# A layer's closing stage put under a written engine order, with two smaller moves of one product and one weight split

## The chip, the cores and the metric

The kernel runs on one core of a Trainium2 chip. The time is the device time of one execution in microseconds; the kernel before takes 1223.93 us (median of 3 runs, 1222.23 to 1228.37).

## What is computed

One layer of a hybrid attention and convolution backbone over 640 tokens of width 1024 (128 context tokens and 512 latent tokens, all float32). The part that matters here is the feed-forward half, with D_FF = 2816:

```python
def conv_ffn(u, p):
    up = dwconv3(u @ p["w_up"], p["conv_ffn"])
    g, val = jnp.split(up, 2, axis=-1)
    return (jax.nn.silu(g) * val) @ p["w_down"]

def trunk_layer(h, ada, p, rope_tabs, ctx_k, ctx_v):
    ...
    h = h + g1 * rms_norm(mo, p["g_post1"])
    u = rms_norm(h, p["g_pre2"]) * (1 + sc2) + sh2
    h = h + g2 * rms_norm(conv_ffn(u, p), p["g_post2"])
    return h, k, v
```

`dwconv3` is a three-tap convolution along the tokens, so an activation tile needs a whole row of tokens. The rest of the layer (modulation, attention, gated convolution, output projection) comes ahead and is the same in both kernels.

## The kernel before, in words

**Products in three parts.** Every large product keeps float32 accuracy by cutting both operands into a high part (a ScalarE copy to a rounded type, `S.activation(..., AF.Copy)`) and a low part (a VectorE subtraction). `mm3` then issues three TensorE matmuls: high by high, high by low, low by high. So every weight tile of 128x1024 costs one ScalarE copy and one VectorE subtraction before TensorE can use it: `split` (L149, L150) for tiles that come through `next_unit`, `hi_of`/`lo_of` (L872, L876) for the w_up tiles, `down_hi`/`down_lo` (L985, L989) for the first 512 columns of w_down, which have one buffer `WD`, and `act_hi`/`act_lo` (L967, L971) for the activations.

**w_up in pairs.** The 2816 columns of each half of w_up are 22 pairs j of 128 columns (NJ = 22). Pairs 0 and 1 are done plainly by `plain(j, tok, i, step)`, 12 matmuls of 322 columns each. Pairs 2 to 21 are done by `strassen(j)` in seven products of 12 matmuls: A11, A12, S2, S1, S3, S4, A22. Two banks of the accumulator memory hold a pair; A22 writes again into the bank of which `added(cv[:, HALF:], j, "p5", 0)` (L931, tile `C`) reads the earlier content, so A22 waits for that VectorE addition.

**Activations, three pairs behind.** While pair j is multiplied, pair j - 3 goes through `tap_mid` (ScalarE, L948), two `taps_out` (VectorE, L953, two instructions each), `silu` (ScalarE), `gated` (VectorE, L962, which also stores the product tile to the DRAM tensor `actd`), `act_hi` and `act_lo`. The high and low parts live in a ring of four tiles (`ACTa`, `ACTb`).

**w_down, first half of the columns.** `down(k)` multiplies activation tile k by its rows of w_down for output columns 0 to 511, 15 matmuls of 512 columns (five token tiles, three matmuls each) in five banks. It runs one pair of w_up later than the activation is made, between S1 and S3. `WD` holds two k at a time and is filled on odd pairs behind S3; the first fill stands in pair 3.

**w_down, second half.** Columns 512 to 1023 need all 22 activation tiles again. Tiles 18 to 21 are still in the ring (`again(i, ts)`, three matmuls per token tile); tiles 0 to 17 are read back from `actd` into `AFB` (eight slots, `act_fetch`) and cut again by `act_of` into `AHB` (L1288) and `ALB` (L1289). The w_down tiles for it (list `rest`) come through `next_unit`. `finish(0, t)` squares and scales the first half of the columns, `finish(1, t)` the second, adds the two sums of squares, takes the inverse root on GpSimd (L1304) and writes the output.

**What sets the order.** From the end of the mixer on, the order of TensorE, ScalarE and VectorE is the order in which the program is written (`manual_schedule`, entered in the ExitStack `fixed`). `fixed.close()` ends this ahead of the loop over tiles 0 to 17; what stands behind it is ordered by a scheduler, which may put its instructions ahead of ones that were written earlier. The queue of SyncE, which issues nearly all DMAs, is ordered by the scheduler throughout. Where the text speaks of a queue, it means an engine's instructions in the order of the built program.

The two remaining places: `turn2(4, hf)` (L822) transposes the last normalised token tile `TX`, and `modulated(4, hf)` scales it into the right-hand operands `B12` and `B22` of the second half of the tokens; `B11` and `B21`, the first half, are complete by then.

Of the kernel before, what the change touches and what calls it, by code (L numbers as in the profile page):

```python
# [11 lines left out]
F32 = mybir.dt.float32  # L12
F32R = mybir.dt.float32r
AF = mybir.ActivationFunctionType
ALU = mybir.AluOpType
AX = mybir.AxisListType

D = 1024
# [3 lines left out]
NT = 5  # L22
# [49 lines left out]
def trunk_layer(ctx, tc, x_prompt, x_sample, cache_k, cache_v, c, c_ctx, w_ada, b_ada, g_pre1, g_post1, g_pre2,  # L72
# [71 lines left out]
    def split(raw):  # L144

        n = raw.shape[1]
        hi = wp.tile([128, 1024], F32R, tag="whi", name=nm("whi"), bufs=3)
        lo = wp.tile([128, 1024], F32R, tag="wlo", name=nm("wlo"), bufs=3)
        S.activation(hi[:, :n], raw, AF.Copy)  # L149
        V.tensor_tensor(out=lo[:, :n], in0=raw, in1=hi[:, :n].bitcast(F32), op=ALU.subtract)  # L150
        return hi, lo

    def fetch(i):
        while len(state["raw"]) < min(i, len(units)):
            w, k0, nk, c0, n = units[len(state["raw"])]
            raw = raw_tile()
            nc.sync.dma_start(raw[:, :nk * n].rearrange("p (k c) -> p k c", c=n),
                              w[k0 * 128:(k0 + nk) * 128, c0:c0 + n].rearrange("(k p) c -> p k c", p=128))
            state["raw"].append(raw)

    def next_unit():
        i = state["next"]
        state["next"] += 1
        fetch(i + 3)
        while len(state["cut"]) < min(i + 2, len(units)):
            w, k0, nk, c0, n = units[len(state["cut"])]
            raw = state["raw"][len(state["cut"])]
            state["cut"].append(Unit(split(raw[:, :nk * n]), n))
        return state["cut"][i]

    def mm3(out, ah, al, bh, bl, start, stop):
# [647 lines left out]
    def turn2(t, hf):  # L819
        p = turned[t, hf] = bank((t, 5 if t == 0 else t - 1)[hf])  # L820
        for k in range(4):
            PE.transpose(p[:, k * 128:(k + 1) * 128], TX[:, t % 2, (4 * hf + k) * 128:(4 * hf + k + 1) * 128], ident)  # L822
# [72 lines left out]
    def plain(j, tok, i, step):  # L895

        if step == 0:
            plain_out[j, tok, i] = bank(PLAIN_BANKS[j, tok, i])[:, 0:HALF]
        block(plain_out[j, tok, i], (j, i), step, f"B{step + 1}{tok + 1}", step == 0, step == 1)
# [46 lines left out]
    def tap_mid(j, i):  # L946
        y, o = acts(j)[0][i], i * NJ + j
        S.activation(y, crows(j)[i][:, 1:1 + NACT], AF.Copy, scale=cffn[:, 44 + o:45 + o])  # L948

    def taps_out(j, i):  # L950
        y, o = acts(j)[0][i], i * NJ + j
        for d in (0, 2):
            V.scalar_tensor_tensor(out=y, in0=crows(j)[i][:, d:d + NACT], scalar=cffn[:, 44 * d + o:44 * d + o + 1], in1=y,  # L953
                                   op0=ALU.mult, op1=ALU.add)

    def silu(j):
        y = acts(j)[0][0]
        S.activation(y, y, AF.Silu)

    def gated(j):  # L960
        ys = acts(j)[0]
        V.tensor_tensor(out=ys[0], in0=ys[0], in1=ys[1], op=ALU.mult)  # L962
        nc.sync.dma_start(actd[j], ys[0])

    def act_hi(j):
        ys, parts = acts(j)
        S.activation(parts[0], ys[0], AF.Copy)  # L967

    def act_lo(j):
        ys, parts = acts(j)  # L970
        V.tensor_tensor(out=parts[1], in0=ys[0], in1=parts[0].bitcast(F32), op=ALU.subtract)  # L971
# [15 lines left out]
    def down_lo(q):  # L987
        hi, lo = (room["wd"][:, i, :] for i in range(2))
        V.tensor_tensor(out=lo, in0=dn["raw"][q], in1=hi.bitcast(F32), op=ALU.subtract)  # L989
# [12 lines left out]
    def strassen(j):  # L1002

        f, nxt = j - FLAG, j + 1 if j + 1 < NJ else None
        g = NJ - FLAG if nxt is None else None
        cg, cv = crows(j)
        pair[j] = tuple(bank(n)[:, 0:HALF] for n in BANKS[j])
        if j > NPLAIN:
            last_copy(j - 1)
        else:  # L1010
            plain_copy(1, 1, 1)
        if f >= 0:
            tap_mid(f, 0)
        lo_of((j, 1))
        product(j, "A11")

        copied(j, "p1", 0)
        if f >= 0:
            tap_mid(f, 1)
            taps_out(f, 0)  # L1020
        product(j, "A12")

        hi_of((j, 2), left(j, 2))
        added(cg[:, 0:HALF], j, "p1", 1)
        lo_of((j, 2))
        product(j, "S2")

        copied(j, "u2", 0)
        if f >= 0:
            silu(f)  # L1030
            taps_out(f, 1)
        product(j, "S1")

        copied(j, "p5", 1)
        hi_of((j, 3), left(j, 3))
        if f >= 0:
            gated(f)
        lo_of((j, 3))
        if nxt:
            adds = sums(nxt)  # L1040
            adds[0]()
        if g:
            tap_mid(g, 0)
            tap_mid(g, 1)
        if j >= DLAG:
            down(j - DLAG)
        product(j, "S3")

        if nxt:
            pair_load(j + 2)  # L1050
            hi_of((nxt, 0), left(nxt, 0))
            lo_of((nxt, 0))
        q = (j - DLAG + 1) // 2
        if j >= DLAG - 1 and (j - DLAG) % 2 == 1:
            down_hi(q)
            down_lo(q)
            down_load(q + 2 if q else 1)
            if q == 0:
                down_load(2)
        added(cv[:, HALF:], j, "p5", 0)  # L1060
        if nxt:
            adds[1]()
        if f >= 0:
            act_hi(f)
        if g:
            taps_out(g, 0)
            silu(g)
        product(j, "S4")

        if nxt:  # L1070
            hi_of((nxt, 1), left(nxt, 1))
        added(cg[:, HALF:], j, "u2", 1)
        if nxt:
            adds[2]()
        if f >= 0:
            act_lo(f)
        if g:
            taps_out(g, 1)
            gated(g)
            act_hi(g)  # L1080
            act_lo(g)
        product(j, "A22")

    def last_copy(j):
        S.activation(crows(j)[1][:, 0:HALF], pair[j][0], AF.Copy)
# [122 lines left out]
    normed(4)  # L1208
    right_hi("B12", "12", 0, 192)
    plain(0, 0, 1, 1)  # L1210
    turn2(4, 0)
    modulated(4, 0)
    right_lo("B22", "22", 0, 192)
# [1 line left out]
    modulated(4, 1)  # L1215
    pair_load(2)
    pair_load(3)
    plain(1, 0, 0, 0)
    right_lo("B12", "12", 0, 192)
    right_hi("B12", "12", 192, HALF)  # L1220
    right_hi("B22", "22", 192, HALF)
# [42 lines left out]
    down_load(0)  # L1264
    plain(1, 1, 1, 1)
    for j in range(NPLAIN, NJ):
        strassen(j)


# [23 lines left out]
    def finish(n, t, pm):  # L1293
        row = 1 if t == 0 else 0
        cs = slice(n * 512, (n + 1) * 512)
        S.activation(JK[:, t % 2, :], pm, AF.Square, accum_out=ssqs[:, t, n:n + 1])
        V.tensor_tensor(out=EX[:, t, cs], in0=pm, in1=G2[:, row, cs], op=ALU.mult)
        first, second = ssqs[:, t, 0:1], ssqs[:, t, 1:2]
        if n == 0:
            V.tensor_scalar(out=first, in0=first, scalar1=D * EPS, scalar2=None, op0=ALU.add)  # L1300
            nc.sync.dma_start(room["h"][:, t, :], hd[t])
            return
        V.tensor_tensor(out=second, in0=second, in1=first, op=ALU.add)  # L1303
        G.tensor_tensor(out=second, in0=second, in1=mhalf[:, 0:1], op=ALU.pow)  # L1304
        for i in range(2):
            cs = slice(i * 512, (i + 1) * 512)
            V.scalar_tensor_tensor(out=EX[:, t, cs], in0=EX[:, t, cs], scalar=second, in1=room["h"][:, t, cs], op0=ALU.mult, op1=ALU.add)
            nc.sync.dma_start(yrows(t)[:, cs], EX[:, t, cs])

    def ending(f):  # L1310

        tap_mid(f, 0)
        tap_mid(f, 1)
        taps_out(f, 0)
        silu(f)
        taps_out(f, 1)
        gated(f)
        act_hi(f)
        act_lo(f)


    units += rest
    pms = [bank(b) for b in RING if b not in BANKS[NJ - 1]]
    us = []

# [3 lines left out]
        for t in ts:  # L1329
            wd_step(pms[t], t, acts(k)[1], us[i // 2].at(i % 2), i == 0, False)  # L1330

    last_copy(NJ - 1)
    ending(NJ - 2)
    fetch(state["next"] + 3)
    down(NJ - 4)
    down(NJ - 3)
    us.append(next_unit())
    pms += [bank(b) for b in BANKS[NJ - 1]]
    again(0, range(3))
    down_hi(NJ // 2 - 1)  # L1340
    down_lo(NJ // 2 - 1)
    again(1, range(3))
    ending(NJ - 1)
    down(NJ - 2)
    us.append(next_unit())
    again(2, range(3))
    act_fetch(5)
    for row in range(2):
        bload(G2[:, row, :], 3, row)
    down(NJ - 1)  # L1350
    again(3, range(3))
    room["h"] = region(ra, "r3", [NT, D], F32, "HX")
    for t in range(NT):
        finish(0, t, dn["pms"][t])
        if t == 1:
            pms += [bank(b) for b in DBANKS[:2]]
            for i in range(4):
                again(i, (3, 4))
    fixed.close()
    NU, tail, av = NJ // 2 - 2, 3, {}  # L1360
    for q in range(NU):
        us.append(next_unit())
        for k in (2 * q, 2 * q + 1):
# [4 lines left out]
    for t in range(NT):  # L1368
        for k in range(2 * (NU - tail), 2 * NU):
            wd_step(pms[t], t, av[k], us[2 + k // 2].at(k % 2), False, k == 2 * NU - 1)  # L1370
        finish(1, t, pms[t])


# [27 lines left out]
```

## Time and profile before

| what | value |
|---|---|
| runs | 1222.23, 1223.93, 1228.37 us |
| the profiled execution, its own time | 1227.19 us |
| its span, first to last instruction | 1225.4 us |
| TensorE busy | 1188.6 us (97%) |
| VectorE, ScalarE, GpSimd busy | 685.1, 526.6, 151.8 us |
| DMA | 130.39 MB, 106 GB/s over the span |

A row of the timeline gives the start, the duration, the engine, the line and the operation, out<-in by tile names; `[x <-E]` behind it says that the engine stood idle for x us before and what ended that. A matmul row's duration runs to the end of its pipeline, so that matmuls which follow each other overlap; the distance between two starts is what one costs. In the view of stretches the column PEclk is the share of full speed that the TensorE clock was granted.

### The profile page before, as it was taken

Reading aid. Unit: us, or ns where it says so; the run is one execution under the profiler, and the core shown is the slowest. Engines: PE = TensorE matmul, PEld = TensorE weight load, DVE = VectorE, ACT = ScalarE, POOL = GpSimd, SP = SyncE. Lnnn points to the kernel's source line nnn. Section 1 sums busy time; section 2 is a strip of 40 time slices with the busy share of each in tenths; the row PEclk is TensorE's granted clock in tenths of the full one; section 3 lists DMA queues with packets and bytes.
Section 4 is the critical chain, followed back from the end, with each engine's and each line's share of the span. In section 5 each row is a group of like instructions: output and inputs, shape, how many; then the busy total and the mean of one; then the engine's idle time right before and its main releaser. Section 6 shows DMA issues by size and latency. Waiting matters only on the chain. (4 is left out here: it accounts for less than half of the span.)

```text
span 1225.4 us, 19707 instructions
## 1 busy us (share of the span) xinstructions
PE 1188.6 (97%) x8109; PEld 1089.1 (89%) x8109; DVE 685.1 (56%) x1091; ACT 526.6 (43%) x896; POOL 151.8 (12%) x188
## 2 busy tenths in 40 slices
PE   6999999999999999999999999989999999997997
PEld 5788888877999999999999987989999999995886
DVE  4486666555122234343333336787888888887443
ACT  4276666665221122222222226555555555555331
POOL 1045556554000000000000003000000000000001
PEclk7998999999999999999999999999999999998999
DMA  8834223144122222222222263333333333316622
GB/s 260 247 112 118 74 70 104 36 121 122 55 70 80 75 70 83 73 70 86 70 70 86 72 202 122 121 100 89 108 105 95 104 100 108 108 57 256 210 63 86
DMA packets 180936, 130.39 MB, mean 106 GB/s; under 512 B 6322, under 2 KB 162542, under 8 KB 180846
## 3 DMA queue, kind: packets, MB, share of 16 engines
q1 hardware_dynamic: 180062, 128.83, 35.0%
q8 instruction: 64, 1.05, 0.4%
q10 hardware_dynamic: 784, 0.30, 0.1%
q14 instruction: 26, 0.21, 0.1%
HBM read 116.34 MB, written 12.77 MB: 105 GB/s over the span
## 5 line engine op out<-in xcount | busy, mean ns | idle before, releaser
L885 PE MATMUL b<-ZB,whi 128*128 128x322 f32 x1024 | 228.2, 310 | 0.0
L149 ACT ACTIVATE whi<-raw 128x1024 fp32r<-128x1024 f32 (+1 forms) x87 | 88.5, 1018 | 317.4 <-PE s L173 166.9
L172 PE MATMUL s<-UH,whi 128*128 128x320 f32 x640 | 198.2, 310 | 0.5 <-ACT PT L588 0.5
L174 PE MATMUL s<-UH,wlo 128*128 128x320 f32 x640 | 197.2, 308 | 0.0
L173 PE MATMUL s<-UL,whi 128*128 128x320 f32 x640 | 197.2, 308 | 0.0
L150 DVE TENSOR_TENSOR wlo<-raw,whi 128x1024 fp32r<-128x1024 f32 (+1 forms) x87 | 102.5, 1179 | 162.4 <-ACT whi L149 160.3
L885 PEld LDWEIGHTS b<-ZB,whi 128*128 128x128 f32 x1024 | 173.7, 189 | 1.6
L885 PE MATMUL b<-ZB,wlo 128*128 128x322 f32 x512 | 159.1, 311 | 0.0
L172 PEld LDWEIGHTS s<-UH,whi 128*128 128x128 f32 x640 | 120.1, 188 | 1.5 <-issue 0.8
L174 PEld LDWEIGHTS s<-UH,wlo 128*128 128x128 f32 x640 | 120.1, 188 | 0.4 <-issue 0.4
L173 PEld LDWEIGHTS s<-UL,whi 128*128 128x128 f32 x640 | 120.1, 188 | 0.0
L885 PEld LDWEIGHTS b<-ZB,wlo 128*128 128x128 f32 x512 | 96.2, 188 | 0.0
L563 POOL TENSOR_TENSOR pr<-pr,sm 128x640 f32<-128x640 f32 x64 | 80.1, 1256 | 67.2 <-DVE sm L561 57.7
L953 DVE SCALAR_TENSOR_TENSOR Y<-C,cffn,Y 128x642 f32<-128x642 f32 x88 | 77.8, 886 | 3.5 <-ACT Y L948 1.8
L872 ACT ACTIVATE whi<-SUM 128x1024 fp32r<-128x1024 f32 x40 | 42.2, 1055 | 59.8 <-PE b L885 53.9
L172 PE MATMUL s<-whi,UH 128*128 128x256 f32 (+1 forms) x200 | 64.5, 322 | 2.6 <-ACT UH L355 1.7
L560 ACT ACTIVATE pr<-s,mx,rq 128x640 f32<-128x640 f32 x64 | 56.6, 885 | 16.5 <-DVE mx L557 14.5
L555 DVE TENSOR_REDUCE mx<-s 128x1 f32<-128x640 f32 x64 | 52.4, 821 | 19.9 <-PE s L552 19.5
L173 PE MATMUL s<-wlo,UH 128*128 128x256 f32 (+1 forms) x200 | 63.1, 316 | 0.0
L174 PE MATMUL s<-whi,UL 128*128 128x256 f32 (+1 forms) x200 | 61.3, 319 | 0.0
L1304 POOL TENSOR_TENSOR ssqs<-ssqs,mhalf 128x1 f32<-128x1 f32 x5 | 3.2, 638 | 444.3 <-DVE ssqs L1303 444.3
L172 PE MATMUL b<-WD,ACTa 128*128 128x512 f32 x110 | 44.5, 405 | 4.8 <-ACT ACTa L967 4.8
(282 smaller groups left out, 2523.5 us busy)
## 6 DMA issues: line engine op xcount, KB each, us to landing
raw<-in_w_in_dram SPq DMA_DIRECT2D x48, 512.0 KB, 3.7
RAW<-in_w_up_dram SPq DMA_DIRECT2D x40, 512.0 KB, 4.1
raw<-in_w_ada_dram SPq DMA_DIRECT2D x32, 512.0 KB, 4.0
raw<-in_w_down_dram SPq DMA_DIRECT2D x22, 512.0 KB, 3.7
araw<-in_w_ada_dram SPq DMA_DIRECT2D x16, 512.0 KB, 7.3
actd<-Y SPq DMA_DIRECT2D x22, 321.0 KB, 3.7
AFB<-actd SPq DMA_DIRECT2D x18, 321.0 KB
raw<-in_w_att_out_dram SPq DMA_DIRECT2D x8, 512.0 KB, 4.0
```

Source lines behind the costliest of these rows:

```text
L149: S.activation(hi[:, :n], raw, AF.Copy)
L150: V.tensor_tensor(out=lo[:, :n], in0=raw, in1=hi[:, :n].bitcast(F32), op=ALU.subtract)
L172: PE.matmul(out, ah, bh, start=start, stop=False)
L173: PE.matmul(out, ah, bl, start=False, stop=False)
L174: PE.matmul(out, al, bh, start=False, stop=stop)
L555: V.tensor_reduce(out=mx, in_=sv, axis=AX.X, op=ALU.max, negate=True)
L560: S.activation(pr, sv, AF.Exp, bias=mx, scale=rs, accum_out=sm)
L563: G.tensor_tensor(out=pr, in0=pr, in1=sm.broadcast_to((128, NTOK)), op=ALU.mult)
L872: S.activation(to[0], raw, AF.Copy)
L885: PE.matmul(out, p[:, ws], q[:, k, :], start=start and k == 0 and n == 0, stop=stop and k == 3 and n == 2, skip_group_check=True)
L953: V.scalar_tensor_tensor(out=y, in0=crows(j)[i][:, d:d + NACT], scalar=cffn[:, 44 * d + o:44 * d + o + 1], in1=y, op0=ALU.mult, op1=ALU.add)
L1304: G.tensor_tensor(out=second, in0=second, in1=mhalf[:, 0:1], op=ALU.pow)
```

## The change

1. `fixed.close()` moves to the very end, so that the closing stage runs in written order on TensorE, ScalarE and VectorE. The written order is laid out anew: the steps of `ending(20)` and `ending(21)` are interleaved by hand with `down(18)` to `down(21)`, `again` and the w_down splits, and the first cut of `AHB` comes behind `finish(0, 1)`.
2. The w_down reloads of `rest` start in pair 21: one is split there (`cut_upto`), the next behind the taps of tile 20.
3. Activation tiles 18 to 21 are no longer stored to `actd` (they were never read back).
4. The sum of the two sums of squares in `finish(1, t)` goes from VectorE to GpSimd.
5. The first filling of `WD` moves from pair 3 to pair 2, with the two loads that follow it.
6. `plain(1, 0, 0, 0)` moves from behind to ahead of the transposes of token tile 4.

```diff
+    def cut_upto(m):
+        while len(state["cut"]) < min(m, len(units)):
+            w, k0, nk, c0, n = units[len(state["cut"])]
+            raw = state["raw"][len(state["cut"])]
+            state["cut"].append(Unit(split(raw[:, :nk * n]), n))
+
     def next_unit():
         i = state["next"]
         state["next"] += 1
         fetch(i + 3)
-        while len(state["cut"]) < min(i + 2, len(units)):
...
+        cut_upto(i + 2)
         return state["cut"][i]
...
     def gated(j):
         ys = acts(j)[0]
         V.tensor_tensor(out=ys[0], in0=ys[0], in1=ys[1], op=ALU.mult)
-        nc.sync.dma_start(actd[j], ys[0])
+        if j < NJ - 4:
+            nc.sync.dma_start(actd[j], ys[0])
...
         if g:
+            cut_upto(len(state["cut"]) + 1)
             tap_mid(g, 0)
             tap_mid(g, 1)
...
-        q = (j - DLAG + 1) // 2
-        if j >= DLAG - 1 and (j - DLAG) % 2 == 1:
+        q = max((j - DLAG + 1) // 2, 0)
+        if j == NPLAIN or (j > DLAG and (j - DLAG) % 2 == 1):
             down_hi(q)
             down_lo(q)
             down_load(q + 2 if q else 1)
...
     plain(0, 0, 1, 1)
+    plain(1, 0, 0, 0)
     turn2(4, 0)
     modulated(4, 0)
...
     pair_load(3)
-    plain(1, 0, 0, 0)
     right_lo("B12", "12", 0, 192)
...
     for j in range(NPLAIN, NJ):
+        if j == NJ - 1:
+            units += rest
+            fetch(state["next"] + 2)
         strassen(j)
...
-        V.tensor_tensor(out=second, in0=second, in1=first, op=ALU.add)
+        G.tensor_tensor(out=second, in0=second, in1=first, op=ALU.add)
         G.tensor_tensor(out=second, in0=second, in1=mhalf[:, 0:1], op=ALU.pow)
...
-    last_copy(NJ - 1)
-    ending(NJ - 2)
-    fetch(state["next"] + 3)
+    act_fetch(5)
+    for row in range(2):
+        bload(G2[:, row, :], 3, row)
+    x, y = NJ - 2, NJ - 1
+    last_copy(y)
+    tap_mid(x, 0)
+    tap_mid(x, 1)
+    taps_out(x, 0)
+    us.append(next_unit())
+    silu(x)
+    taps_out(x, 1)
     down(NJ - 4)
+    gated(x)
+    act_hi(x)
+    act_lo(x)
     down(NJ - 3)
-    us.append(next_unit())
+    tap_mid(y, 0)
+    tap_mid(y, 1)
     pms += [bank(b) for b in BANKS[NJ - 1]]
     again(0, range(3))
     down_hi(NJ // 2 - 1)
     down_lo(NJ // 2 - 1)
+    taps_out(y, 0)
+    silu(y)
     again(1, range(3))
-    ending(NJ - 1)
-    down(NJ - 2)
+    taps_out(y, 1)
+    down(x)
+    gated(y)
+    act_hi(y)
+    act_lo(y)
     us.append(next_unit())
     again(2, range(3))
-    act_fetch(5)
-    for row in range(2):
-        bload(G2[:, row, :], 3, row)
-    down(NJ - 1)
+    room["h"] = region(ra, "r3", [NT, D], F32, "HX")
+    down(y)
     again(3, range(3))
-    room["h"] = region(ra, "r3", [NT, D], F32, "HX")
     for t in range(NT):
         finish(0, t, dn["pms"][t])
         if t == 1:
             pms += [bank(b) for b in DBANKS[:2]]
             for i in range(4):
                 again(i, (3, 4))
-    fixed.close()
-    NU, tail, av = NJ // 2 - 2, 3, {}
+            av[0] = act_of(0)
...
         finish(1, t, pms[t])
+    fixed.close()
```

`ending(f)`, which the change removes, was `tap_mid(f, 0)`, `tap_mid(f, 1)`, `taps_out(f, 0)`, `silu(f)`, `taps_out(f, 1)`, `gated(f)`, `act_hi(f)`, `act_lo(f)` in this order.

More of the change, by code (lines that the diff above doesn't have):

```diff
@@ L164, in next_unit @@
         fetch(i + 3)
-        while len(state["cut"]) < min(i + 2, len(units)):
-            w, k0, nk, c0, n = units[len(state["cut"])]
-            raw = state["raw"][len(state["cut"])]
-            state["cut"].append(Unit(split(raw[:, :nk * n]), n))
+        cut_upto(i + 2)
         return state["cut"][i]
@@ L1308, in finish @@
             nc.sync.dma_start(yrows(t)[:, cs], EX[:, t, cs])
[L1310 to L1322, printed above, removed]
     pms = [bank(b) for b in RING if b not in BANKS[NJ - 1]]
@@ L1341, in trunk_layer @@
     down_lo(NJ // 2 - 1)
+    taps_out(y, 0)
+    silu(y)
     again(1, range(3))
-    ending(NJ - 1)
-    down(NJ - 2)
+    taps_out(y, 1)
[3 more added lines that the diff above has]
+    act_lo(y)
     us.append(next_unit())
     again(2, range(3))
-    act_fetch(5)
-    for row in range(2):
-        bload(G2[:, row, :], 3, row)
-    down(NJ - 1)
+    room["h"] = region(ra, "r3", [NT, D], F32, "HX")
+    down(y)
     again(3, range(3))
-    room["h"] = region(ra, "r3", [NT, D], F32, "HX")
+    NU, tail, av = NJ // 2 - 2, 3, {}
     for t in range(NT):
```

## The prediction

> **What bounds the kernel now.** I read the page first, then the view of waits for TensorE, then its timeline around each wait, then the timelines of the engine that ended it.
>
> ```profile
> PE 1188.6 (97%) x8109; PEld 1089.1 (89%) x8109; DVE 685.1 (56%) x1091; ACT 526.6 (43%) x896; POOL 151.8 (12%) x188
> ```
>
> TensorE is busy for 97% of the span, and the change takes no matmul away. So only its idle time, and time in which it runs at a lower clock, can be won. The waits of TensorE, over the whole span (total, times, longest):
>
> ```profile
> PE b L172 <- ACT ACTa L967: 4.8, 1, 4.8
> PE b L885 <- DVE C L931: 3.7, 2, 2.7
> ...
> PE b L172 <- ACT whi L149: 2.6, 1, 2.6
> PE b L822 <- DVE TX L813: 2.4, 2, 1.8
> ```
>
> All four rows lie where the change acts: the first and third in the closing stage, the second in pairs 2 and 3, the fourth at the transposes of token tile 4. The TensorE timeline gives places, and the view of stretches the granted clock (PEclk) around three of them and one other:
>
> ```profile
> 774.37 1.09 PE L822 MATMUL b<-ident,TX 128*128 128x128 f32 x8 [1.81 <-DVE TX L813]
> ...
> 808.45 0.54 PE L885 MATMUL b<-ZT,whi 128*128 128x322 f32 x2 [0.99 <-DVE C L931]
> ...
> 823.89 0.88 PE L885 MATMUL b<-ZT,whi 128*128 128x322 f32 x2 [2.74 <-DVE C L931]
> ...
> 827.25 0.49 PE L885 MATMUL b<-ZB,whi 128*128 128x322 f32 x2
> ...
> 1114.12 0.39 PE L172 MATMUL b<-WD,ACTa 128*128 128x512 f32 x1
> ...
> 1122.71 0.79 PE L172 MATMUL b<-WD,ACTa 128*128 128x512 f32 x1 [4.84 <-ACT ACTa L967]
> ...
> 1131.59 0.79 PE L172 MATMUL b<-whi,ACTa 128*128 128x512 f32 x1 [2.56 <-ACT whi L149]
> ...
> 1139.19 0.39 PE L172 MATMUL b<-WD,ACTa 128*128 128x512 f32 x1
> ...
> 1150.36 0.39 PE L172 MATMUL b<-whi,AHB 128*128 128x512 f32 x1
> ```
>
> ```profile
> 774.00:776.00 2.00, 1.63 (x13) 1.64 (x14) 0.31 (x1) 0.94 (x3) 0.00 (x0) 1.00 0.86 310
> ...
> 823.00:825.00 2.00, 1.11 (x4) 1.14 (x5) 2.00 (x5) 0.54 (x1) 0.00 (x0) 0.72 0.59 144
> ...
> 1120.00:1122.00 2.00, 0.00 (x0) 0.00 (x0) 2.00 (x4) 1.84 (x4) 0.00 (x0) 0.71 0.99 379
> ...
> 1130.00:1132.00 2.00, 0.41 (x1) 0.29 (x1) 1.25 (x2) 2.00 (x3) 0.00 (x0) 0.77 0.89 342
> ```
>
> The gaps of 2.74, 4.84 and 2.56 us are followed by a clock of a half (a mean of 0.72 in 823 to 825 is a fall from 1.0 to 0.5 inside it); the gap of 1.81 us is not (1.00).
>
> **The closing stage.** Between 1114.12 and 1150.36 stand `down(18)` to `down(21)` and 36 matmuls of `again`: 4 x 15 + 36 = 96 matmuls in 36.24 us. From 1139.19 to 1150.36 the last 48 run without a wait: 11.17 / 48 = 0.233 us each. So 96 need 22.3 us and 13.9 are lost: 4.8 and 2.6 in the two waits of the table, the rest, 6.5, by the clock and short waits behind it. Why the waits are there is read from ScalarE:
>
> ```profile
> 1113.78 0.74 ACT L1288 ACTIVATE AHB<-AFB 128x642 fp32r<-128x642 f32 x1 [3.12 <-DMA AFB<-actd]
> ...
> 1118.73 3.18 ACT L1288 ACTIVATE AHB<-AFB 128x642 fp32r<-128x642 f32 x4 [2.94 <-DMA AFB<-actd]
> 1121.92 0.74 ACT L967 ACTIVATE ACTa<-Y 128x642 fp32r<-128x642 f32 x1
> ```
>
> The scheduler put cuts of reloaded tiles (`AHB`) ahead of tile 19's own; they wait for DMAs, and `silu(19)` and `ACTa` of tile 19 stand behind them. In the built order of the changed kernel no `AHB` stands ahead of `finish(0, 0)`, and ahead of pair 21 the only moves are those of pairs 2 and 3 and token tile 4. So the DMA waits go; late next is the work on tiles 20 and 21 itself. I walk it with these means (stretch 1104 to 1151, lines grouped); a successor on the same engine starts some 0.08 us before the row ahead of it ends.
>
> ```profile
> L953 DVE SCALAR_TENSOR_TENSOR Y<-C,cffn,Y 128x642 f32<-128x642 f32 x14 | 12.2, 883 | 0.2
> ...
> L948 ACT ACTIVATE Y<-C,cffn 128x642 f32<-128x642 f32 x6 | 4.6, 820 | 0.0
> ...
> L150 DVE TENSOR_TENSOR wlo<-raw,whi 128x1024 fp32r<-128x1024 f32 x3 | 3.6, 1223 | 0.2
> ...
> L971 DVE TENSOR_TENSOR ACTb<-Y,ACTa 128x642 fp32r<-128x642 f32 x4 | 3.3, 824 | 1.6 <-ACT ACTa L967 1.6
> ...
> L149 ACT ACTIVATE whi<-raw 128x1024 fp32r<-128x1024 f32 x3 | 3.0, 1041 | 0.0
> ...
> L967 ACT ACTIVATE ACTa<-Y 128x642 fp32r<-128x642 f32 x4 | 2.9, 735 | 5.1 <-DVE Y L962 5.1
> ...
> L989 DVE TENSOR_TENSOR WD<-raw,WD 128x1024 fp32r<-128x1024 f32 x2 | 2.4, 1222 | 2.9 <-ACT WD L985 2.9
> L985 ACT ACTIVATE WD<-raw 128x1024 fp32r<-128x1024 f32 x2 | 2.1, 1052 | 1.1 <-PE b L174 1.1
> ```
>
> ```profile
> 1111.61 1.80 DVE L953 SCALAR_TENSOR_TENSOR Y<-C,cffn,Y 128x642 f32<-128x642 f32 x2
> ```
>
> VectorE reaches the taps of tile 19 at 1111.61 as before: the new split in pair 21 (1.04 on ScalarE, 1.22 on VectorE) fits into the time in which both wait for `down(17)` to free `WD`. Then: two taps to 1113.4, one short addition and `ACTb` of tile 18 to 1114.55, two taps to 1116.3, the product (`gated`, as long as `ACTb`) to 1117.0; `ACTa` of tile 19 at 1117.8, `ACTb` at 1118.65. ScalarE goes on with the copy of pair 21 (some 0.4) and the two middle taps of tile 20 (1119.6) and the second split (1120.6). VectorE: taps to 1120.7, split 1121.85, taps 1123.55, product 1124.3. ScalarE: `ACTa` of tile 20 at 1125.1, two middle taps of tile 21 to 1126.5, `WD` at 1127.5; VectorE's half of `WD` at 1128.8, four taps of tile 21 to 1132.2, product 1132.95, `ACTa` 1133.7, `ACTb` 1134.6.
>
> TensorE against this: `down(18)` ends at 1117.6; `down(19)` waits 0.2 for `ACTa` and 0.4 for `ACTb`; with 18 matmuls of `again` it is through at 1125.9 and waits 1.6 for `WD`'s high part, runs one matmul, and waits 1.1 for the low part. `down(21)` comes at 1134.1, after its `ACTa`. So 3.3 us of waiting stay, and 22.3 + 3.3 = 25.6 against 36.24 is a gain of 10.6. The pair 1.6 + 1.1 is nearest to the row at 1131.59 (2.56), which lost the clock; I charge one loss of the size of the row at 823.89: 12 matmuls of 322 columns took 3.36 us until 827.25, against 84 in 12.44 at full clock,
>
> ```profile
> 1013.32 12.44 PE b L885 x84
> ```
>
> which is 1.78 for 12: 1.6 us. **Closing stage: -9.0** (from -10.6 without a loss to -7.4 with 3.2, half of the 6.5 that two gaps cost before).
>
> **Behind it.** In written order the last w_down split stands ahead of the cuts of tiles 15 to 17, and it waits until the matmuls of tile 11 have freed its buffer: 1.04 + 1.22 for the split, then `ALB` of tile 15 (as long as `ACTb`) at 2.3 + 0.8 = 3.1 us, where TensorE, at 0.7 us a tile, wants it 2.5 us after tile 11: with two short waits for tiles 16 and 17 it is **+0.8** (0 to 1.5). At the very end the addition goes from VectorE (behind the `EX` product) to GpSimd, which can start when ScalarE has its sum:
>
> ```profile
> 1219.41 0.19 ACT L1296 ACTIVATION_READ_ACCUMULATOR JK<-b 128x1 f32 x1
> ```
>
> ```profile
> 1220.25 0.15 DVE L1303 TENSOR_TENSOR ssqs<-ssqs 128x1 f32<-128x1 f32 x1
> ```
>
> ```profile
> 1220.48 0.55 POOL L1304 TENSOR_TENSOR ssqs<-ssqs,mhalf 128x1 f32<-128x1 f32 x1 [3.64 <-DVE ssqs L1303]
> ```
>
> ```profile
> L796 POOL TENSOR_TENSOR root<-ssq x5: 194/195/394, 739.4 to 765.0; 128x1 f32<-128x1 f32 x5
> ```
>
> ScalarE's sum is there at 1219.6, so GpSimd's two steps end at 1220.4 instead of 1221.0: **-0.5** (0 to -0.6). The four stores of `actd` that go leave SyncE's queue; nothing waited for them: 0.
>
> **Pairs 2 and 3.** In pair 3 VectorE does `WD` ahead of the addition that A22 waits for:
>
> ```profile
> 822.12 1.22 DVE L989 TENSOR_TENSOR WD<-raw,WD 128x1024 fp32r<-128x1024 f32 x1
> 823.26 0.48 DVE L931 TENSOR_TENSOR C<-b,p 128x322 f32<-128x322 f32 x1
> ```
>
> Starts are 1.14 us apart. Moved to pair 2, which has no `taps_out` yet but a wait of 0.99 at the same place, it makes that 2.13 and this 1.60: no gain in waiting. What can go is the loss of clock behind the 2.74: both new gaps are nearer to 1.81, which lost none, than to 2.56. **-1.6** (from -1.6 to +1.6, if both lose it).
>
> **Token tile 4.** `plain(1, 0, 0, 0)`, 12 matmuls, 1.78 us, goes into the wait of 1.81 for `TX`. Its weights' low part and, behind the transposes, the right-hand operands for the second half of the tokens are VectorE's:
>
> ```profile
> 770.53 2.56 DVE L876 TENSOR_TENSOR wlo<-raw,whi 128x1024 fp32r<-128x1024 f32 x2
> ...
> 778.09 1.56 DVE L753 TENSOR_TENSOR ZB<-UFa,ZB 128x768 fp32r<-128x768 f32 x2
> ```
>
> The first low part ends at 771.8, in time for 772.4. `B12` is complete at 779.65; TensorE will come to it at 775.2 + 3 x 1.78 = 780.6, so the cover of 3.6 us from the two plain products left behind shrinks to 0.9, but holds. **-1.8** (0 if a wait of the same length comes up later).
>
> **Sum.** -9.0 + 0.8 - 0.5 - 1.6 - 1.8 = -12.1 us against the profiled execution (span 1225.4, own time 1227.19): span 1213, own time 1215. The median of the runs is 1223.93, 3.3 lower; taken off it the same sum gives 1211.8. Part of the 3.3 may be clock that the median run didn't lose, so I give **1212.5**.
>
> **The rivals.**
> First, no clock is lost at the new gaps. For it: none is as long as 2.56. Against: the two behind `again` are split by one matmul alone. The sum is then 1.6 lower: 1210.9. [...]
>
> [...]
>
> Third, the chain of taps is longer than I walk it, or the fourth place gives its time back, so that only the first of the two waits and its clock go (4.8 + 3.2, less some 3 that come up again): -5, 1219, within 0.5%.
>
> Fourth, slower: the reload of `G2` takes the place of `AFB`'s. `G2`'s two DMAs now stand in SyncE's queue behind a w_down load that waits for `WD`'s low part (1128.8). `finish(0, 0)` and `finish(0, 1)` need them, and `again` for token tiles 3 and 4 needs the banks these free, from 1139.7 on; VectorE's later splits queue behind them.
>
> ```profile
> G<-bct SPq DMA_DIRECT2D x2, 512.0 KB, 8.0
> ```
>
> With 8.0 us to land they are there at some 1138, and the two products end by 1139.5. From then on each us of delay costs one; the gain of 12 is used up at some 20 us to landing, and it is slower by over 0.5%, about what a measurement of this kernel can tell from no change, from 26 on: 1230. Against: the 8.0 were measured with the reloads of `AFB` ahead, of which only one is now.
>
> That the change does not do what it says is excluded by the built order.
>
> **Chances.** Forecast 0.48, no loss 0.20, more loss 0.20, little 0.08, slower 0.04. The first three are all over 0.5% (6.1 us) faster: 0.88; the others 0.08 and 0.04. With the bounds of the terms the first three span 1208 to 1217.5.
>
> **What would show it.** Right: no `AHB` on ScalarE ahead of the first `JK`; from `down(18)`'s first matmul to the first `AHB` matmul, less the 24 of `again` that now come ahead of it, some 27 us; waits of TensorE for `WD`, of 1 to 2 us, in place of those for `ACTa` and `whi`; 2.1 and 1.6 before A22 in pairs 2 and 3; no wait at L822's last call; 0.5 to 0.8 before tile 15. Wrong: a wait for L1305 (`EX`) on TensorE, a wait of VectorE for `G`, or the plain products of the second half of the tokens waiting for `ZB`.

## The result, and the profile after

| | before | after |
|---|---|---|
| median of the runs | 1224.54 us (4 runs, 1222.23 to 1228.37) | 1212.76 us (4 runs, 1212.30 to 1214.20) |
| ratio, 95% interval | | 0.9903 (0.9876 to 0.9930) |
| the profiled execution, its own time | 1227.19 us | 1214.20 us |
| its span | 1225.4 us | 1212.4 us |

The changed kernel is 11.8 us faster by the medians, 13.0 by the spans of the two profiled executions. The forecast was 1212.5 us. Line numbers after the change are three or four higher in the functions named so far (L885 is L888, L172 to L174 are L175 to L177, L967 is L971), the same in `split` (L149, L150), and eight higher from L1288 on.

The busy times on the page of the profile after:

```profile
PE 1182.6 (98%) x8109; PEld 1083.8 (89%) x8109; DVE 684.1 (56%) x1086; ACT 524.9 (43%) x896; POOL 152.0 (13%) x193
```

TensorE has the same 8109 matmuls. Its busy time is 6.0 us shorter, since more of them ran at full clock (the mean over the span is 0.992 against 0.984); 2.0 us of that lie in the start, which the change does not touch. Its waits after the change, in the view of waits for TensorE (total, times, longest):

```profile
PE b L888 <- DVE C L934: 3.7, 2, 2.1
...
PE b L175 <- ACT WD L989: 1.5, 1, 1.5
...
PE b L176 <- DVE WD L993: 0.8, 1, 0.8
PE b L177 <- DVE ALB L1297: 0.6, 1, 0.6
PE b L825 <- DVE TX L816: 0.6, 1, 0.6
```

The row for `C` keeps its total of 3.7 and has another split (2.1 and 1.6 for 2.7 and 1.0). Of the 4.8 for `ACTa` 0.15 is left, and the 2.6 for `whi` is gone. In their place stand 1.5 and 0.8 for `WD`, and a new 0.6 for `ALB`. Of the two waits for `TX`, the one of 1.8 is gone. The timeline of TensorE has them in their places:

```profile
772.46 1.09 PE L825 MATMUL b<-ident,TX 128*128 128x128 f32 x8
...
805.94 0.54 PE L888 MATMUL b<-ZT,whi 128*128 128x322 f32 x2 [2.12 <-DVE C L934]
...
821.72 0.54 PE L888 MATMUL b<-ZT,whi 128*128 128x322 f32 x2 [1.60 <-DVE C L934]
...
1110.46 0.39 PE L175 MATMUL b<-WD,ACTa 128*128 128x512 f32 x1
...
1114.36 0.50 PE L175 MATMUL b<-WD,ACTa 128*128 128x512 f32 x1 [0.15 <-ACT ACTa L971]
...
1124.21 0.49 PE L175 MATMUL b<-WD,ACTa 128*128 128x512 f32 x1 [1.50 <-ACT WD L989]
1125.47 0.50 PE L176 MATMUL b<-WD,ACTa 128*128 128x512 f32 x1 [0.77 <-DVE WD L993]
...
1136.77 0.39 PE L175 MATMUL b<-whi,ACTa 128*128 128x512 f32 x1
```

The row at 1110.46 is the first matmul of `down(18)`; the row at 1136.77 is the 97th from there. So the 96 matmuls that took 36.24 us before take 26.31. The view of stretches has the clock (PEclk, third from the right) at the new gaps:

```profile
803.80:809.80 6.00, 3.88 (x17) 3.89 (x17) 4.82 (x7) 1.89 (x3) 0.00 (x0) 0.74 0.61 178
820.10:825.10 5.00, 3.40 (x24) 3.41 (x24) 5.00 (x8) 2.22 (x3) 0.00 (x0) 1.00 0.54 133
1122.70:1128.70 6.00, 3.73 (x16) 2.85 (x16) 4.44 (x5) 2.20 (x3) 0.00 (x0) 1.00 0.31 86
```

Each stretch begins where its gap does. The clock fell at the 2.12 of pair 2, and neither at the 1.60 of pair 3 nor at the pair of gaps in the closing stage.

From such landmarks the span can be cut into six stretches that every kernel here has. "First transposes" is the call of L822 (L825 after) for the first four transposes of `TX`, `down(0)` the first matmul of that step:

| us | before | after | difference |
|---|---|---|---|
| start to the first transposes | 745.30 | 743.39 | -1.9 |
| from there to `down(0)` (holds token tile 4 and pairs 2, 3) | 89.07 | 87.32 | -1.75 |
| `down(0)` to `down(18)` | 279.75 | 279.75 | 0 |
| 96 matmuls from `down(18)` | 36.24 | 26.31 | -9.93 |
| the 97th to the last matmul | 68.07 | 68.99 | +0.92 |
| the last matmul to the end | 6.97 | 6.64 | -0.33 |

The first row is not the change's: nothing is edited there. Over the eleven profiles of this study that stretch lies between 742.2 and 745.3 us, and the clock goes with it: its mean over the first 105 us is 0.90 in the longest (the kernel before) and 0.95 in the shortest (`cuts_first`). Here are the first 30 us before, and then after:

```profile
0.00:30.00 30.00, 19.98 (x160) 16.08 (x161) 13.85 (x30) 13.56 (x25) 5.62 (x18) 0.81 0.87 258
```

```profile
0.00:30.00 30.00, 19.89 (x162) 16.32 (x163) 13.88 (x30) 13.57 (x25) 5.42 (x18) 0.86 0.85 257
```

Nearly the same work, at a mean clock of 0.81 in one execution and 0.86 in the other. So stages are compared by stretches below, and whole times only where there are several runs.

### The profile page after: what moved, and what is told of

It reads as the page before. It is cut to its first block, busy times and chain, and to the rows that moved or that the text cites. A ratio compares the mean times of both kernels' runs of the same rounds, so it can differ in the third digit from the quotient of the medians.

```text
span 1212.4 us, 19701 instructions
## 1 busy us (share of the span) xinstructions
PE 1182.6 (98%) x8109; PEld 1083.8 (89%) x8109; DVE 684.1 (56%) x1086; ACT 524.9 (43%) x896; POOL 152.0 (13%) x193
## 5 line engine op out<-in xcount | busy, mean ns | idle before, releaser
L149 ACT ACTIVATE whi<-raw 128x1024 fp32r<-128x1024 f32 (+1 forms) x87 | 88.7, 1019 | 338.6 <-PE s L176 166.9
L888 PE MATMUL b<-ZB,whi 128*128 128x322 f32 x1024 | 228.7, 311 | 0.0
L150 DVE TENSOR_TENSOR wlo<-raw,whi 128x1024 fp32r<-128x1024 f32 (+1 forms) x87 | 102.4, 1177 | 180.0 <-ACT whi L149 175.4
L175 PE MATMUL s<-UH,whi 128*128 128x320 f32 x640 | 198.3, 310 | 0.5 <-ACT PT L591 0.5
L177 PE MATMUL s<-UH,wlo 128*128 128x320 f32 x640 | 197.4, 308 | 0.0
L888 PEld LDWEIGHTS b<-ZB,whi 128*128 128x128 f32 x1024 | 174.2, 190 | 1.6
L888 PE MATMUL b<-ZB,wlo 128*128 128x322 f32 x512 | 159.4, 311 | 0.0
L175 PEld LDWEIGHTS s<-UH,whi 128*128 128x128 f32 x640 | 120.2, 188 | 1.5 <-issue 0.8
L177 PEld LDWEIGHTS s<-UH,wlo 128*128 128x128 f32 x640 | 120.2, 188 | 0.4 <-issue 0.4
L888 PEld LDWEIGHTS b<-ZB,wlo 128*128 128x128 f32 x512 | 96.6, 189 | 0.0
L175 PE MATMUL s<-whi,UH 128*128 128x256 f32 (+1 forms) x200 | 63.9, 319 | 2.6 <-ACT UH L358 1.7
L177 PE MATMUL s<-whi,UL 128*128 128x256 f32 (+1 forms) x200 | 60.4, 314 | 0.0
```

What stands on the lines that cost most here:

```text
L175: PE.matmul(out, ah, bh, start=start, stop=False)
L177: PE.matmul(out, al, bh, start=False, stop=stop)
L888: PE.matmul(out, p[:, ws], q[:, k, :], start=start and k == 0 and n == 0, stop=stop and k == 3 and n == 2, skip_group_check=True)
```

## The experiments

The runs of the kernel before beside them have medians of 1225.42 us (26 runs; the first four experiments), 1224.86 us (9 runs; the next four) and 1225.09 us (one run; the last).

### The closing stage without the two early moves

The changed kernel with parts 5 and 6 undone (`tail_only`):

```diff
     plain(0, 0, 1, 1)
-    plain(1, 0, 0, 0)
     turn2(4, 0)
...
     pair_load(3)
+    plain(1, 0, 0, 0)
...
-        q = max((j - DLAG + 1) // 2, 0)
-        if j == NPLAIN or (j > DLAG and (j - DLAG) % 2 == 1):
+        q = (j - DLAG + 1) // 2
+        if j >= DLAG - 1 and (j - DLAG) % 2 == 1:
```

> The closing stage as in the changed kernel, pairs 2 and 3 and token tile 4 as before. If the closing stage carries the gain: the 96 matmuls from down(18) on in 26.3 us as in the changed kernel (28 to 29.5 if the clock falls at the two gaps of 1.5 and 0.8), in all 8.5 to 10 us faster than the kernel before. If the moves in pairs 2 and 3 and at token tile 4 carried it, 2 us or less.

Measured: 1216.91 us (4 runs), ratio 0.9918 (0.9901 to 0.9936): 8.5 us faster by the medians, 10.0 by the ratio. The 96 matmuls take 27.58 us. The waits in them are those of the changed kernel (0.16, 1.49, 0.76), but the clock fell behind them:

```profile
1126.10:1132.10 6.00, 3.78 (x9) 2.82 (x10) 4.48 (x5) 2.15 (x3) 0.00 (x0) 0.72 0.29 87
```

So the closing stage carries most of the gain, and the loss of clock that the forecast charged there is paid in some executions (this one, 1.3 us) and not in others.

### The written order's end alone

The kernel before with nothing but `fixed.close()` moved (`close_only`):

```diff
-    fixed.close()
     NU, tail, av = NJ // 2 - 2, 3, {}
...
         finish(1, t, pms[t])
+    fixed.close()
```

> The kernel before with fixed.close() alone moved to the end: written order, but the old layout with ending(20) whole, all four stores kept. Theory (the scheduler's early AHB cuts, waiting for DMAs on ScalarE, were the loss): no AHB ahead of the first JK, the waits for AFB gone; new waits of 4.0 and 1.0 us at again(0), because both w_down splits stand behind ending(20), and a fallen clock behind them; 96 matmuls in some 28 without and 30 to 31 us with it, the kernel 5 to 7.5 us faster than before. Rival 1 (the interleaving by hand carries it): within 2 us of before. Rival 2 (the four stores and the DMA load carry it): within 2 us of before as well, with the waits for AFB still there.

Measured: 1222.34 us (7 runs), ratio 0.9969 (0.9959 to 0.9980): 3.1 us faster by the medians, 3.8 by the ratio, less than was expected. The 96 matmuls take 29.75 us; the next stretch is 1.1 longer (69.13). The timelines of ScalarE and TensorE:

```profile
1122.52 0.74 ACT L967 ACTIVATE ACTa<-Y 128x642 fp32r<-128x642 f32 x1 [1.91 <-DVE Y L962]
1123.16 1.99 ACT L149 ACTIVATE whi<-raw 128x1024 fp32r<-128x1024 f32 x2
...
1138.11 0.60 ACT L1296 ACTIVATE JK<-b 128x512 f32<-128x512 f32 x1 [4.28 <-PE b L174]
...
1146.79 1.99 ACT L1288 ACTIVATE AHB<-AFB 128x642 fp32r<-128x642 f32 x3
```

```profile
1124.25 0.80 PE L172 MATMUL b<-whi,ACTa 128*128 128x512 f32 x1 [3.11 <-ACT whi L149]
1125.51 0.80 PE L173 MATMUL b<-wlo,ACTa 128*128 128x512 f32 x1 [0.46 <-DVE wlo L150]
```

No `AHB` stands ahead of the first `JK` any more, and the wait of 4.84 for `ACTa` is down to 0.17: the scheduler's hoist was its cause. But in the old written order both splits (1.99 for their two high parts) stand behind the `ACTa` of tile 20, which ends at 1123.2, and TensorE waits 3.11 for the first, with a mean clock of 0.68 in the 6 us from the start of that wait. Moving the end of the written order is worth 6.5 us in that stretch against the profile before, and 5.0 and 6.0 against the two other profiles of the old closing stage (34.77 us in `tile4_only`, 35.77 in `wd_pair2_only`), 3 to 4 in all; the rest of the change's closing gain comes from the new interleaving, which puts one split into pair 21 and one between the taps.

### The product ahead of the transposes alone

The kernel before with part 6 alone (`tile4_only`):

```diff
     plain(0, 0, 1, 1)
+    plain(1, 0, 0, 0)
     turn2(4, 0)
...
-    plain(1, 0, 0, 0)
```

> The kernel before with plain(1,0,0,0) ahead of the transposes of token tile 4. Theory: the wait of 1.81 us there goes and does not come up again, -1.8 us. Rival (the cover behind it is used up and a wait of the same length comes at the plain products of the second half): 0.

Measured: 1223.35 us (12 runs), ratio 0.9984 (0.9973 to 0.9996): 2.1 us faster. The stretch from the transposes to `down(0)` takes 87.34 us against 89.07: -1.73, nearly the length of the wait. It does not come up again later.

### The first w_down split alone

The kernel before with part 5 alone (`wd_pair2_only`):

```diff
-        q = (j - DLAG + 1) // 2
-        if j >= DLAG - 1 and (j - DLAG) % 2 == 1:
+        q = max((j - DLAG + 1) // 2, 0)
+        if j == NPLAIN or (j > DLAG and (j - DLAG) % 2 == 1):
```

> The kernel before with the first filling of WD in pair 2 alone. Theory: waits of 2.13 and 1.60 in place of 0.99 and 2.74, sum unchanged at 3.73; the clock falls behind at most one of them, so 0, with -1.6 or +1.6 by chance of the run. Rival (it saves the clock for good): -1.6 in the median and a clock of 1.00 behind both in the profile.

Measured: 1224.6 us (12 runs), ratio 0.9994 (0.9984 to 1.0004): nothing that can be told from no change. The stretch takes 89.08 us against 89.07. The clock behind the two gaps:

```profile
805.80:811.80 6.00, 3.87 (x17) 3.90 (x17) 4.82 (x7) 1.56 (x3) 0.00 (x0) 0.72 0.63 175
822.10:827.10 5.00, 3.40 (x24) 3.41 (x24) 5.00 (x8) 2.23 (x3) 0.00 (x0) 1.00 0.53 137
```

The waits are 2.13 and 1.60, as worked out. The loss behind the 2.74 of pair 3 is gone, and one behind the 2.13 of pair 2 has come.

### The last filling of WD earlier

In the changed kernel TensorE waits for `WD` because its high part stands on ScalarE behind `ACTa` of tile 20 and the middle taps of tile 21. Here (`wd_early`) it comes as soon as `down(19)` has read the buffer:

```diff
     down(NJ - 4)
-    gated(x)
-    act_hi(x)
-    act_lo(x)
     down(NJ - 3)
+    down_hi(NJ // 2 - 1)
+    gated(x)
+    down_lo(NJ // 2 - 1)
+    act_hi(x)
+    act_lo(x)
     tap_mid(y, 0)
     tap_mid(y, 1)
     pms += [bank(b) for b in BANKS[NJ - 1]]
     again(0, range(3))
-    down_hi(NJ // 2 - 1)
-    down_lo(NJ // 2 - 1)
```

> The changed kernel with the last filling of WD written ahead of the activation split of tile 20 (its high part right behind down(19), its low part between the product of tile 20 and ACTb). Theory (in the closing stage the waits of 1.5 and 0.8 us are the written place of WD behind the middle taps of tile 21, not work that must come first): both go, ACTb of tile 20 comes 0.3 us later at most, the 96 matmuls take 23.3 to 24 us instead of 26.3, the kernel 2.3 to 3 us faster than the changed one, some 1210. Rival (VectorE's chain of taps is the bound, so the time comes up again at down(21)): 96 matmuls in 25.5 or more, with a wait for ACTa at down(21).

Measured: the 96 matmuls take 23.75 us, with no wait left but the 0.15 for `ACTa`; by ScalarE's timeline the high part runs 4.4 us earlier than after the change:

```profile
1118.68 1.06 ACT L989 ACTIVATE WD<-raw 128x1024 fp32r<-128x1024 f32 x1 [0.58 <-PE b L177]
```

The median is 1211.89 us (4 runs, ratio 0.9891, 0.9873 to 0.9909), only 0.9 below the changed kernel's. The profiled execution is 2.4 below (span 1210.0), although its first stretch is 1.6 longer: beside the 2.6 of the closing stage it took 1.5 less in pairs 2 and 3, where no clock was lost in this execution. With four runs of each and a start that varies by 3 us from one execution to the next, the medians cannot tell 1 us from 2.5 here; the stretch can.

### The last cuts ahead of the last split

In the changed kernel the last w_down split waits for its buffer and the cuts of tiles 15 to 17 queue behind it. Here (`cuts_first`) they come ahead:

```diff
     for q in range(NU):
+        if q == NU - 2:
+            for k in range(2 * q, 2 * NU):
+                av[k] = act_of(k)
         us.append(next_unit())
```

> The changed kernel with the cuts of tiles 14 to 17 written ahead of the last w_down split. Theory: the wait of 0.58 us for ALB goes, the matmuls from the 97th of the closing stage to the last take 68.1 us as before instead of 69.0, and the split itself, needed 2.8 us after its buffer is free, does not come late: 0.8 us faster than the changed kernel. Rival (the split then comes late by as much): 0, with a wait for wlo.

Measured: 68.09 us from the 97th to the last matmul, against 68.99 after and 68.07 before, and no wait for `ALB`. ScalarE's timeline after the change, and then here:

```profile
1184.27 1.06 ACT L149 ACTIVATE whi<-raw 128x1024 fp32r<-128x1024 f32 x1 [4.62 <-PE b L177]
1185.24 1.98 ACT L1296 ACTIVATE AHB<-AFB 128x642 fp32r<-128x642 f32 x3
```

```profile
1177.05 3.24 ACT L1296 ACTIVATE AHB<-AFB 128x642 fp32r<-128x642 f32 x5
1183.03 1.06 ACT L149 ACTIVATE whi<-raw 128x1024 fp32r<-128x1024 f32 x1 [2.73 <-PE b L177]
```

The one run took 1212.02 us. So the +0.92 is the place of those cuts behind the waiting split and nothing else.

### The addition ahead of the next pair's weights

A22 of pairs 2 and 3 waits for a VectorE addition of 0.48 us that stands behind the low parts for the next pair and, in one of them, behind `WD`. Here (`add_first`) it goes ahead of them in these pairs:

```diff
+        early = j <= NPLAIN + 1
+        if early:
+            added(cv[:, HALF:], j, "p5", 0)
         if nxt:
             pair_load(j + 2)
             hi_of((nxt, 0), left(nxt, 0))
...
-        added(cv[:, HALF:], j, "p5", 0)
+        if not early:
+            added(cv[:, HALF:], j, "p5", 0)
```

> The changed kernel with the addition that A22 waits for written ahead of the cuts for the next pair, in pairs 2 and 3 alone. Theory (VectorE's order, not its load, makes the waits of 2.13 and 1.60 us): they fall to some 0.1 and 0.5, no clock is lost there, and from the first transposes to down(0) it takes 82.5 to 84 us instead of 87.3; 3 to 4.5 us faster than the changed kernel. Rival (pairs 2 and 3 are bound by VectorE's load at the start of the pairs): the waits come up at A11 or S2 of the next pair, 0 to 1 us.

Measured: the stretch from the transposes to `down(0)` takes 83.18 us against 87.32, as expected; gaps of 0.46 and 0.47 are left. The median is 1212.28 us (4 runs, ratio 0.9890, 0.9870 to 0.9910), 0.5 below the changed kernel's, not the 3 to 4.5 expected. In the profiled execution some of the gain was lost elsewhere: the start took 1.55 us longer than in the changed kernel's profile, and behind the gaps of 1.50 and 0.77 in the closing stage, the same as there, the clock fell (96 matmuls in 27.65 us):

```profile
1120.10:1126.10 6.00, 3.74 (x11) 2.73 (x11) 4.42 (x5) 2.21 (x3) 0.00 (x0) 0.79 0.28 88
```

### The three together

The edits of the last three kernels in one (`all_three`).

> The three last edits together on the changed kernel. Each acts in its own stage, so the gains add: 6 to 8.5 us faster than the changed kernel, 1204 to 1207.

Measured: 1206.66 us (5 runs, 1205.86 to 1208.08), ratio 0.9854 (0.9836 to 0.9872): 6.1 us below the changed kernel and 18 below the kernel before. The stretches are those of the single edits: 83.17, 23.75 and 68.09 us. Against the changed kernel that is 7.6 us less in these three, and the start is 0.7 shorter: the span of 1204.1 is 8.3 shorter, and the median shows 6.1 of it. In these stretches no gap of over 0.5 us is left behind the transposes. This is the fastest version here.

### The stores and the addition put back

The changed kernel with parts 3 and 4 undone (`stores_and_add_back`). The edit adds four stores, those of tiles 18 to 21, which makes 22; the other 18 are in the changed kernel too, and are read.

```diff
-        if j < NJ - 4:
-            nc.sync.dma_start(actd[j], ys[0])
+        nc.sync.dma_start(actd[j], ys[0])
...
-        G.tensor_tensor(out=second, in0=second, in1=first, op=ALU.add)
+        V.tensor_tensor(out=second, in0=second, in1=first, op=ALU.add)
```

> The changed kernel with the 22 stores of the activation (the actd array that nothing reads) back, and with the last-stage addition of the squared sums back on VectorE instead of GpSimd. If those edits only shorten the end by the addition's place, the 96 matmuls of the closing stage stay at 26.3 us (26.1 to 26.6), and the stretch from the last matmul's start to the span's end goes from 6.64 back to about 6.97 us: +0.3 in all. If the stores had cost transfer time behind which the last w_down loads waited, the 96 matmuls take 27.5 us or more (where the clock stays at 1.00). If both are nothing, the last stretch stays at 6.6.

Measured: one run of 1216.27 us, span 1214.5. Lines of the functions behind L966 are one lower here than after the change. The last stretch is 6.99 us against 6.64: the addition's place is worth the 0.35 us. But the 96 matmuls take 28.97 us, 2.66 more than after the change, and not for a late w_down load. The timelines of SyncE's queue and of ScalarE:

```profile
1120.11 0.32 SPq L966 DMA_DIRECT2D actd<-Y  x1
```

```profile
1120.11 0.74 ACT L970 ACTIVATE ACTa<-Y 128x642 fp32r<-128x642 f32 x1 [3.04 <-DVE Y L965]
1122.16 1.55 ACT L951 ACTIVATE Y<-C,cffn 128x642 f32<-128x642 f32 x2 [1.31 <-DMA actd<-Y]
1123.62 1.04 ACT L988 ACTIVATE WD<-raw 128x1024 fp32r<-128x1024 f32 x1
```

The store of tile 20 is still reading `Y` when ScalarE comes to the middle taps of tile 21, which write into it. They wait 1.31 us, `WD`'s high part stands behind them, and TensorE's wait for it grows from 1.50 to 2.92. The clock fell behind that gap, as the view of stretches shows:

```profile
1122.80:1128.80 6.00, 3.33 (x8) 2.44 (x9) 4.04 (x5) 2.60 (x4) 0.00 (x0) 0.75 0.26 91
```

So in this execution the dead stores cost 1.4 us of waiting, and a loss of clock of some 1.2 beside it. That is neither of the two theories but a third, seen in one execution.

## Why the prediction was right, and where it was not

**The closing stage** was forecast at -9.0 and came out at -9.93. The mechanism is shown: the hoisted cuts caused the wait for `ACTa` (the written order's end alone removes it), and the waits that take its place are those of the walk. It gave 0.2, 0.4, 1.6 and 1.1; the rows show 0.15, 1.50 and 0.77, and a start 0.29 us late for `ACTb`. Shifted by the 3.66 us by which `down(18)` comes earlier, the walk has `WD`'s high part done at 1123.84 and its low part at 1125.14; in the trace they end at 1124.16 and 1125.41:

```profile
1123.12 1.04 ACT L989 ACTIVATE WD<-raw 128x1024 fp32r<-128x1024 f32 x1
```

```profile
1124.19 1.22 DVE L993 TENSOR_TENSOR WD<-raw,WD 128x1024 fp32r<-128x1024 f32 x1 [1.56 <-ACT WD L989]
```

The term that was off is the clock loss of 1.6, which this execution did not pay. It was a charge for an even chance: of the four profiles with exactly these two gaps, two lost clock there. So the -9.93 is in part chance too. The old closing stage took 34.77, 35.77 and 36.24 us in the three profiles that have it, the new one 26.29, 26.31, 27.58 and 27.65 in its four; the difference of the means is 8.6 us.

**Pairs 2 and 3** were forecast at -1.6 and gave nothing. The gaps came out as worked out, 2.12 and 1.60. The step that failed is "both new gaps are nearer to 1.81, which lost none, than to 2.56": behind 2.13 the clock fell in three of five profiles, so the loss moved from one pair to the other. Nearness to a gap that lost none was the wrong measure: the 1.81 lost none in each of its four profiles, and 2.13 is nearer to it than to 2.56. The term's own bound of +1.6, for a loss behind both gaps, was kept in the range.

**Token tile 4** was forecast at -1.8: -1.73 alone, -1.75 for the stretch of the full change. The cover of 0.9 us held; no wait for `ZB` appeared.

**Behind the closing stage** +0.8 was forecast and +0.92 measured, with the wait of 0.58 for `ALB` that was named; taking the cuts ahead removes it. For the addition on GpSimd -0.5 was forecast and -0.33 measured (-0.35 when undone). The two steps on GpSimd came as forecast:

```profile
1207.01 0.19 POOL L1311 TENSOR_TENSOR ssqs<-ssqs 128x1 f32<-128x1 f32 x1 [3.38 <-ACT JK L1304]
1207.28 0.55 POOL L1312 TENSOR_TENSOR ssqs<-ssqs,mhalf 128x1 f32<-128x1 f32 x1
```

VectorE's last products follow them. Their row before, and then after:

```profile
1221.06 1.41 DVE L1307 SCALAR_TENSOR_TENSOR EX<-EX,ssqs,HX 128x512 f32<-128x512 f32 x2 [0.66 <-POOL ssqs L1304]
```

```profile
1207.86 1.41 DVE L1315 SCALAR_TENSOR_TENSOR EX<-EX,ssqs,HX 128x512 f32<-128x512 f32 x2 [0.21 <-POOL ssqs L1312]
```

They start 2.10 us behind the last matmul's start (1205.76) where it was 2.63 (1218.43): -0.53. From their end to the span's end it is 3.1 us where it was 2.9, so 0.2 was given back in the last output stores; what made these later stays open.

**The stores** were forecast at 0 because "nothing waited for them". That holds for the order before, where the reason was read. In the new order it fails: there the stores cost 1.4 us of waiting in the one profile that has them back. It did not move the forecast, since the walk of the closing stage had no store in it; so the -9.93 holds this part too.

**The fourth rival's** premise was wrong. It put `G2`'s DMAs behind a w_down load that waits for `WD`'s low part. On SyncE's queue they were issued at 1110.71, behind a w_down load at 1109.36 that went out long before that low part. The load that does wait for it stands behind them, at 1125.44, just after the low part ends (1125.41):

```profile
1109.36 0.74 SPq L157 DMA_DIRECT2D raw<-in_w_down_dram  x1
...
1110.71 1.07 SPq L760 DMA_DIRECT2D G<-bct  x2
...
1125.44 0.38 SPq L157 DMA_DIRECT2D raw<-in_w_down_dram  x1
```

TensorE has no wait for `EX` and VectorE none for `G`. So the case did not arise, because the order of that queue is not the one that the text assumed.

**The sum** was -12.1 against the profiled execution, and -13.0 came: -1.75 - 9.93 + 0.92 - 0.33 = -11.1 from the change, and -1.9 from the start, which the change does not touch. That the median fell within 0.3 us of the forecast is partly luck: two misses, the clock in pairs 2 and 3 (+1.6) and in the closing stage (-0.9), in part offset each other. The range does not follow from the bounds of the terms alone: all at one end, and token tile 4 left at its -1.8, they give 1210.0 or 1218.5 around the 1212.5, where the text has 1208 to 1217.5.

## What to carry to other kernels

Where a scheduler orders an engine's queue, look in the queue ahead of a late instruction for one that waits for a DMA: it holds everything behind it, however early its result is wanted (here TensorE waited 4.84 us for `ACTa`), and a written order removes it only if the steps are also interleaved anew (without that, 3 to 4 us came of the 8.5 to 10). Refill a single buffer directly behind its last reader, put an addition that frees an accumulator bank ahead of work for later, and drop stores that nothing reads, because a store holds its source tile against the next writer (here ScalarE waited 1.31 us for one). The gap of 2.13 us on TensorE cost another 1.5 us in clock in some executions and nothing in others: judge an edit by the stretch it changes in several profiles, and close such gaps rather than move them.

## What the runs showed of the hardware

The clock fell behind every gap of 2.74 us on TensorE here, behind some of those of 2.13 us, and behind some of the pairs of 1.50 and 0.77 us. The mean granted clock in the 5 to 6 us from the start of a gap, over all eleven profiles (a fall is a mean under 0.9):

| gap, us | place | fell |
|---|---|---|
| 0.99 | pair 2, old order | 0 of 4 |
| 1.60 | pair 3, new order | 0 of 5 |
| 1.81 | transposes, old order | 0 of 4 |
| 2.13 | pair 2, new order | 3 of 5 (0.72 to 0.76; the others 1.00) |
| 2.74 | pair 3, old order | 4 of 4 (0.73 to 0.85) |
| 1.50 and 0.77, one matmul between | closing stage | 2 of 4 (0.72, 0.79; the others 1.00) |

The same gap of 2.12, here without a fall (`wd_early`), in the view of stretches:

```profile
805.40:811.40 6.00, 3.88 (x27) 3.89 (x27) 5.42 (x8) 2.22 (x3) 0.00 (x0) 1.00 0.65 180
```

In these 6 us 27 matmuls start there, and 17 after the change: at 0.15 us each, 1.5 us of loss.

The row of that view for the fall after the change, which came 0.7 us behind the end of the gap (805.94), has the clock at 0.50:

```profile
806.63:810.05 3.42, 3.42 (x14) 3.42 (x14) 1.99 (x3) 2.02 (x3) 0.00 (x0) 0.50 0.71 215
```

Ahead of the closing stage `wd_early` has no edit against the changed kernel. So the difference at this gap is one between two executions, not one that the edit makes; what sets it is left open here.
